# DeltaNet's value transposes as fp32r words beside the fp32 ones, with other banks and another order for the fills of a hybrid decoder block

## The chip, the core and the metric

The kernel runs on one NeuronCore of a Trainium2 chip. Its engines are TensorE (PE in the profile, its weight loads PEld), VectorE (DVE), ScalarE (ACT), GpSimd (POOL) and SyncE (SP), which issues all DMAs here. The metric is device time in microseconds (us) of one execution, median of several; lower is better.

## What is computed

One decoder block on x of 1024 tokens by 1024 features, all in float32. Cut to what matters:

```python
h = rmsnorm(x, norm1_w)
proj = h @ w_in                       # 1024 x 4104, columns split among the groups
# 8 heads of 64: strictly causal stick-breaking attention
#   A[t,s] = sigmoid(z_ts) * prod_{s<j<t} (1 - sigmoid(z_tj)),  o = A @ v
# 4 heads of 128: q, k, v = silu(causal conv of 4 taps); q, k l2-normalised;
#   S_t = exp(g_t) S_{t-1} (I - beta_t k_t k_t^T) + beta_t k_t v_t^T ; o_t = S_t^T q_t
mixed = concat(rmsnorm(o_attention) * silu(z), rmsnorm(o_deltanet) * silu(z'))
x = x + mixed @ w_out
return rmsnorm(x, final_norm_w)
```

The DeltaNet part is computed in chunks, here of 128 tokens: a triangular system per chunk is inverted, and a scan over the eight chunks of a head carries the state.

## The kernel before

**Precision and products.** Large products (input and output projections, attention) split each float32 operand into a high part, written as fp32r, and the remainder, also fp32r, and sum three products (`mm3`, L517: high by high, high by low, low by high). DeltaNet's own small products and all transposes are plain fp32.

**Stages in order of time.** First a straight piece of code: attention's q projection (L563 to L589), while x and the weights are loaded, then the row scales `rstd` (L591 to L600), which go to HBM as `rs_s` and come back to all partitions as `rbc`; DVE multiplies the input by it (L615) and ACT and DVE split it anew into `xh` and `xl` (L647 to L649) while PE computes half of the attention's v and DeltaNet's gate inputs (L641 to L646). Then come the interleaved streams, described below, and in the end the output projection (`product`, L1400).

**Streams.** From L1460 the rest of the program is a set of Python generators (class `Stream`, L378): `projections` (the *fills*: 24 weight column blocks, each in two halves of 512 tokens and 24 matmuls a half, with v's second half of heads among them), `delta_pre`, `delta_load`, `delta_solve` and `delta_scan` for DeltaNet, `attention` with a stream for each window of 256 queries, and the preparation and product of the output projection. `ORDER` (L29) is the order of the fills: G0 (DeltaNet head 0: k, q, v columns), v1, G1, k0 and so on. A generator yields a condition, or an operation whose result its next matmuls need.

**Who goes next.** The kernel simulates itself while it is built. `Model` (L132) gives every recorded operation a cost and an end; `interleave` (L392) takes, whenever PE's modelled queue is empty, the ready stream of the lowest number `prio`; fills have 100 and so go only when no chain is ready. A stream is ready (`Stream.ready`, L386) when each operation that it yielded has ended and its result has had time to reach PE: `HOPS` of its engine plus `TO_PE`, 70 ns. Streams other than fills need one free `pz` bank. The other engines' orders come from the same simulation and are written down as dependencies (L1468 to L1471), so that each engine's order is fixed in the program. PE's is that of the program.

**Banks.** PSUM's eight banks have names: two `pp`, one `pc`, four `pz`, one `po` (L442 to L445). A fill's half waits until one of the two `pp` banks is free (`ps.room`, L839), computes into it, and hands it to an eviction. For DeltaNet columns this is `g_evac` (L775): ACT copies the bank to `pre`, ACT and three DVE operations do the convolution, the first steps in the bank itself, the last into a tile `ac` of tag `kt`, of which there are two; then sigmoid, a POOL product, and a DMA to `g_s`. The evictions for k and z columns use the same two `kt` tiles.

**The part that is changed most.** `gdn_pre` (L920) prepares half a head (four chunks): it transposes k and q (L935), computes norms and the two chunk products (L961), and then, when the values `vt` have been loaded from `g_s` (`delta_load`, L900), transposes the four 128x128 blocks of `vt` into one `pz` bank (L975) and lets ACT copy each, scaled, to `nkv` (L977). The scan (`gdn_chain`, L1091) reads `nkv` later.

**Start.** Eight matmuls of the identity run first on PE (L560), and ACT's first instruction is the scaled copy of the first part of x to `xh` (L578).

Of the kernel before, what the change touches and what calls it, by code (L numbers as in the profile page):

```python
# [10 lines left out]
F32 = mybir.dt.float32  # L11
F32R = mybir.dt.float32r
I32 = mybir.dt.int32
AF = mybir.ActivationFunctionType
# [3 lines left out]
P = 128  # L18
# [20 lines left out]
SAME = 130  # L39
HOPS = {"A": 145, "G": 75, "P": 197, "V": 130, "S": 900}  # L40
TO_PE = 70

PORT = 60

# [87 lines left out]
class Model:  # L132
# [102 lines left out]
    def finish(self, op):  # L235
        op.end = self.now
        for u in op.users:
            self.wake(u, op.end + self.hop(op, u))
        self.at(op.end + HOPS[op.eng] + TO_PE, lambda: None)

    def arrive(self, op):
        if op.late:
# [135 lines left out]
class Stream:  # L378
# [7 lines left out]
    def ready(self, ck):  # L386
        if self.gate and not self.gate():
            return False
        return all(o.end is not None and o.end + HOPS[o.eng] + TO_PE <= ck.now for o in self.waits)


def interleave(ck, room, streams):  # L392
# [29 lines left out]
def block(tc, xT_d, x_d, n1_d, wE_d, wQ_d, wC_d, conv_d, alog_d, dtb_d, mixw_d, wo_d, fnw_d, out_d):  # L422
# [4 lines left out]
    with ExitStack() as top:  # L427
# [33 lines left out]

        make_identity(nc, ident)
        V.memset(step[:, 0:384], 0.0)
        rsg = cst.tile([P, GH, NB], F32, name="rsg")
        gsc = {n: cst.tile([P, GH, NB], F32, name=n) for n in ("beta", "cum", "eg", "neg", "egl", "kd")}

# [90 lines left out]
        alog, dtb = sm[:, 692:696], sm[:, 696:700]  # L557
        qp = [pp(), pp(), pz(), pc(), pz(), pz(), pz(), po()]

        for _ in range(8):  # L560
            TE.matmul(qp[7][:, 0:P], ident, ident, start=True, stop=True)
        raw, loads = [], {"n": [S.dma_start(n1, n1_d)]}
# [236 lines left out]
        def projections():  # L799
# [29 lines left out]
            while nxt:  # L829
                name, cols = nxt  # L830
                if name[0] == "v":
                    nxt = take()
                    split(nxt, 2)
                    yield from values()
                    continue
                fill.prio = 100
                for half in range(2):
                    hs = slice(half * 512, (half + 1) * 512)
                    yield lambda: ps.room("pp", 2)  # L839
                    pt = pp()  # L840
                    for k in range(NK):
                        n = 8 * half + k
                        if n == 2:
                            nxt = take()
                        if n == 8:
                            split(nxt, 1)
                        if n == 12:
                            split(nxt, 2)
                        h, l = cols.hl[k // 4]
                        mm3(pt, h[:, k % 4, :], l[:, k % 4, :], xh[:, k, hs], xl[:, k, hs], k == 0, k == NK - 1)  # L850
                        if k < NK - 1:
                            yield
                    if half == 0:
                        if name[0] == "G":
                            ev = g_evac(int(name[1]), int(name[2]))
                        else:
                            ev = {"k": k_evac, "z": z_evac}[name[0]](int(name[1]))
                    flags[name if half else name + ".0"] = ev(pt, half)
                    yield
                if nxt is None:  # L860
                    nxt = take()
                    if nxt is None and todo:
                        yield lambda: any(ok() for _, ok in todo)
                        nxt = take()
                    split(nxt, 2)
# [15 lines left out]
        def delta_load():  # L881
            yield lambda: "dec" in flags
            for h in range(GH):
                for g in range(2):
                    u = 2 * h + g
                    gst[h, g] = {}
                    half = "" if g else ".0"
                    yield lambda: u < 4 or f"c{u - 4}" in flags
                    if u > 3:
                        yield flags[f"c{u - 4}"]  # L890
                    kq = gd.tile([P, 4, 2, P], F32, tag="kq", bufs=4, name="kq")
                    ts = slice(512 * g, 512 * g + 512)
                    loads = []
                    for kind in (1, 0):
                        yield lambda: f"G{h}{kind}{half}" in flags
                        loads.append(S.dma_start(kq[:, :, 1 - kind, :], g_s[h, kind, :, ts].rearrange("p (c t) -> p c t", c=4)))
                    gst[h, g].update(kq=kq)
                    flags[f"l{u}g"] = loads
                    yield lambda: f"G{h}2{half}" in flags and (u == 0 or f"q{u - 1}" in flags)
                    vt = gd.tile([P, 4, P], F32, tag="vt", name="vt")  # L900
                    flags[f"v{u}g"] = S.dma_start(vt.rearrange("p c t -> p (c t)"), g_s[h, 2, :, ts])
                    gst[h, g].update(vt=vt)

        def delta_solve():
# [15 lines left out]
        def gdn_pre(h, g):  # L920
# [51 lines left out]
            vt = st["vt"]  # L972
            tp = pz()
            for j in range(4):
                TE.transpose(tp[:, j * P:(j + 1) * P], vt[:, j, :], ident)  # L975
            for j in range(4):
                A.activation(nkv[:, j, :], tp[:, j * P:(j + 1) * P], AF.Copy, scale=nk[:, j:j + 1])  # L977
            qg = kq[:, :, 1, :]
            flags[f"q{2 * h + g}"] = G.tensor_tensor(qg, qg, cb, ALU.mult)
            yield  # L980
# [524 lines left out]
```

## Time and profile before

| | |
|---|---|
| median of 3 runs | 667.47 us (667.22 to 668.82) |
| the profiled execution | 667.83 us |
| its span, first to last instruction | 666.1 us |
| mean granted TensorE clock | 0.998 |
| HBM read and written | 75.50 and 34.51 MB |

How to read the rows that follow: a row of a timeline has the start in us, the duration, the engine, the line (L312 is the recorder through which almost every instruction passes, so rows are told apart by their tiles), the operation, the output tile, the input tiles, the shape and the count; in brackets stands the idle time of the engine before it and what ended it. A row of groups has the count, then busy us in all and the mean in ns, then idle us before. Matmul durations overlap, since matmuls are pipelined: how long a series takes is read from the distance of starts. fp32r tiles are shown as f32 in PE rows.

### The profile page before, as it was taken

To read this page: it belongs to the slowest core of one execution; us is meant where nothing else is said; L and a number is where in the kernel's file an instruction comes from. 1 tells how busy PE (TensorE), PEld (TensorE's weight loads), DVE (VectorE), ACT (ScalarE), POOL (GpSimd) and SP (SyncE) were. 2 spreads that over 40 slices of the span, in tenths; PEclk is the share of its full clock that TensorE was granted. 3 is DMA by queue.
4 is the path that set the end of the run, shared out by engine and by line. 5 is a ranking of instruction groups with operands and counts; after the bars stand their busy time and mean duration, and the time that the engine had idled before them with its cause. 6 is when DMAs were issued, how large, how long until landed. Compare 5 with 4: busy or idle time off the path is not lost.

```text
span 666.1 us, 11687 instructions
## 1 busy us (share of the span) xinstructions
PE 654.0 (98%) x3990; PEld 559.1 (84%) x3990; DVE 442.7 (66%) x842; ACT 381.6 (57%) x898; POOL 341.5 (51%) x372
## 2 busy tenths in 40 slices
PE   8999999999999999999999999999999999999996
PEld 6889887998888898888888888788988888888885
DVE  4349984525558989855647786888688952977632
ACT  5636557825447878555548685769697832222111
POOL 0106144918675687726784385823455451665411
PEclk9999999999999999999999999999999999999999
DMA  7929346862674265343692525452546633764411
GB/s 297 333 82 362 115 147 220 292 193 80 213 223 143 71 192 148 102 134 117 173 301 81 179 81 144 136 170 72 164 154 229 198 92 123 245 221 159 136 64 63
DMA packets 96331, 110.78 MB, mean 166 GB/s; under 512 B 29520, under 2 KB 61456, under 8 KB 96272
## 3 DMA queue, kind: packets, MB, share of 16 engines
q1 hardware_dynamic: 96272, 110.04, 51.1%
q8 instruction: 31, 0.51, 0.3%
q14 instruction: 28, 0.23, 0.1%
HBM read 75.50 MB, written 34.51 MB: 165 GB/s over the span
## 4 chain that ended last, share of the span: by engine, by line
PE 81%; DMA 5%; DVE 4%; POOL 3%; ACT 2%; issue 2%; SPq 1%; POOLq 0%; ACTq 0%; DVEq 0%
PE pp L312 47%; PE pz L312 25%; PE po L312 6%; PE pc L312 4%; POOL tt L312 1%; DVE xl L312 1%; DMA wcr<-wC 1%; DMA xa<-xd 1%; DMA dt<-cum_s 1%; DVE xr L312 1%; ACT L312 1%; DMA wer<-wE 1%; SPq L312 1%; DMA cb<-cum_s 1%; POOL wel L312 1%
## 5 line engine op out<-in xcount | busy, mean ns | idle before, releaser
L312 PE MATMUL pp<-xh,weh 128*128 128x512 f32 x384 | 159.3, 415 | 1.4 <-DVE ac L312 1.4
L312 PE MATMUL pp<-xh,wel 128*128 128x512 f32 x384 | 150.7, 392 | 0.3 <-POOL wel L312 0.3
L312 PE MATMUL pp<-xl,weh 128*128 128x512 f32 x384 | 150.2, 391 | 0.3 <-DVE xl L312 0.3
L312 POOL TENSOR_TENSOR sg<-sg,cc 128x128 f32<-128x128 f32 (+3 forms) x64 | 79.1, 1239 | 78.0 <-DVE cc L312 73.9
L312 POOL TENSOR_TENSOR wel<-wer,weh 128x512 fp32r<-128x512 f32 x48 | 61.9, 1292 | 50.2 <-ACT weh L312 49.1
L312 PEld LDWEIGHTS pp<-xh,wel 128*128 128x128 f32 x384 | 72.1, 188 | 16.6 <-POOL wel L312 0.7
L312 PEld LDWEIGHTS pp<-xh,weh 128*128 128x128 f32 x384 | 72.4, 189 | 13.1 <-DVE ac L312 2.0
L312 PEld LDWEIGHTS pp<-xl,weh 128*128 128x128 f32 x384 | 72.5, 189 | 11.4 <-DVE xl L312 0.7
L312 DVE TENSOR_TENSOR al<-pz,ah 128x512 fp32r<-128x512 f32 (+1 forms) x80 | 49.6, 630 | 17.1 <-ACT ah L312 16.7
L312 ACT ACTIVATE sg<-pz,rs 128x384 f32<-128x384 f32 (+3 forms) x96 | 53.7, 589 | 7.5 <-PE pz L312 6.4
L312 DVE TENSOR_TENSOR_SCAN cc<-pz,step 128x384 f32<-128x384 f32 (+2 forms) x64 | 53.3, 846 | 6.4 <-ACT pz L312 6.2
L312 DVE SCALAR_TENSOR_TENSOR pp<-pre,conv,pp 128x512 f32<-128x512 f32 x48 | 35.9, 749 | 30.8 <-ACT pp L312 30.4
L312 ACT ACTIVATE ah<-pz 128x512 fp32r<-128x512 f32 (+1 forms) x80 | 43.8, 558 | 20.8 <-PE pz L312 19.5
L312 ACT ACTIVATE pz<-pz,ns 128x384 f32<-128x384 f32 (+3 forms) x96 | 52.8, 568 | 0.0
L312 POOL TENSOR_TENSOR ac<-ac,pre 128x512 f32<-128x512 f32 x24 | 31.1, 1295 | 29.6 <-ACT pre L312 21.6
L312 PE MATMUL pp<-woh,mh 128*128 128x512 f32 (+2 forms) x120 | 46.1, 384 | 0.0
L312 PE MATMUL pp<-woh,ml 128*128 128x512 f32 (+2 forms) x120 | 45.5, 379 | 0.0
L312 PE MATMUL pp<-wol,mh 128*128 128x512 f32 (+2 forms) x120 | 45.3, 378 | 0.0
L312 PE MATMUL pz<-step,sg 128*128 128x128 f32 x288 | 43.9, 275 | 0.1
L312 PE MATMUL po<-ah,v2a 128*128 128x256 f32 (+1 forms) x160 | 42.8, 292 | 0.0
L312 ACT ACTIVATE xr<-y 128x1024 f32<-128x1024 f32 (+3 forms) x10 | 8.9, 889 | 55.8 <-DVE y L312 55.8
L312 DVE TENSOR_TENSOR_SCAN cc<-pz,cc,step 128x512 f32<-128x512 f32 (+1 forms) x32 | 38.7, 1211 | 3.0 <-ACT pz L312 2.3
(252 smaller groups left out, 1593.4 us busy)
## 6 DMA issues: line engine op xcount, KB each, us to landing
wer<-wE SPq DMA_DIRECT2D x48, 256.0 KB, 3.8
xr<-x SPq DMA_DIRECT2D x16, 512.0 KB, 6.1
g_s<-ac SPq DMA_DIRECT2D x24, 256.0 KB, 2.4
v_s<-v2e SPq DMA_DIRECT2D x16, 256.0 KB, 2.6
kq<-g_s SPq DMA_DIRECT2D x16, 256.0 KB, 3.6
v2a<-v_s SPq DMA_DIRECT2D x8, 512.0 KB, 4.2
q<-qk_s SPq DMA_DIRECT2D x8, 512.0 KB, 5.0
kh<-qk_s SPq DMA_DIRECT2D x8, 512.0 KB, 4.9
```

Of the source, the lines that this page charges most:

```text
L312: ins = f(*args, **kw).ins
```

## The change

1. `SLACK = 450` ns is added to the time at which a stream is ready after an operation that it yielded.
2. A tile `idr` holds the identity as fp32r.
3. ACT's first instruction becomes a copy of the small constant `half` into `rs8` (which is written properly later), ahead of the identity matmuls.
4. The second halves of G0's fills take a `pz` bank instead of a `pp` bank.
5. The tile `vt` becomes fp32r. `gdn_pre` transposes its four blocks as fp32r words into one `pz` bank and once more as fp32 into a second one. DVE copies the fp32 result to a tile `tv` (tag `kt`), subtracts it from the fp32r result into the second bank, and adds 2^30 times this difference to `tv`. ACT's four scaled copies read `tv` instead of PSUM.

```diff
--- before.py
+++ after.py
@@ -39,6 +39,7 @@
 SAME = 130
 HOPS = {"A": 145, "G": 75, "P": 197, "V": 130, "S": 900}
 TO_PE = 70
+SLACK = 450
 
 PORT = 60
 
@@ -236,7 +237,7 @@
         op.end = self.now
         for u in op.users:
             self.wake(u, op.end + self.hop(op, u))
-        self.at(op.end + HOPS[op.eng] + TO_PE, lambda: None)
+        self.at(op.end + HOPS[op.eng] + TO_PE + SLACK, lambda: None)
 
     def arrive(self, op):
         if op.late:
@@ -386,7 +387,7 @@
     def ready(self, ck):
         if self.gate and not self.gate():
             return False
-        return all(o.end is not None and o.end + HOPS[o.eng] + TO_PE <= ck.now for o in self.waits)
+        return all(o.end is not None and o.end + HOPS[o.eng] + TO_PE + SLACK <= ck.now for o in self.waits)
 
 
 def interleave(ck, room, streams):
@@ -461,6 +462,8 @@
 
         make_identity(nc, ident)
         V.memset(step[:, 0:384], 0.0)
+        idr = cst.tile([P, P], F32R, name="idr")
+        V.tensor_copy(idr, ident)
         rsg = cst.tile([P, GH, NB], F32, name="rsg")
         gsc = {n: cst.tile([P, GH, NB], F32, name=n) for n in ("beta", "cum", "eg", "neg", "egl", "kd")}
 
@@ -557,6 +560,7 @@
         alog, dtb = sm[:, 692:696], sm[:, 696:700]
         qp = [pp(), pp(), pz(), pc(), pz(), pz(), pz(), po()]
 
+        A.activation(rs8, half, AF.Copy)
         for _ in range(8):
             TE.matmul(qp[7][:, 0:P], ident, ident, start=True, stop=True)
         raw, loads = [], {"n": [S.dma_start(n1, n1_d)]}
@@ -836,8 +840,9 @@
                 fill.prio = 100
                 for half in range(2):
                     hs = slice(half * 512, (half + 1) * 512)
-                    yield lambda: ps.room("pp", 2)
-                    pt = pp()
+                    wide = name[:2] == "G0" and half
+                    yield lambda: ps.room("pz", 4) if wide else ps.room("pp", 2)
+                    pt = pz() if wide else pp()
                     for k in range(NK):
                         n = 8 * half + k
                         if n == 2:
@@ -897,8 +902,8 @@
                     gst[h, g].update(kq=kq)
                     flags[f"l{u}g"] = loads
                     yield lambda: f"G{h}2{half}" in flags and (u == 0 or f"q{u - 1}" in flags)
-                    vt = gd.tile([P, 4, P], F32, tag="vt", name="vt")
-                    flags[f"v{u}g"] = S.dma_start(vt.rearrange("p c t -> p (c t)"), g_s[h, 2, :, ts])
+                    vt = gd.tile([P, 4, P], F32R, tag="vt", name="vt")
+                    flags[f"v{u}g"] = S.dma_start(vt.rearrange("p c t -> p (c t)").bitcast(F32), g_s[h, 2, :, ts])
                     gst[h, g].update(vt=vt)
 
         def delta_solve():
@@ -972,9 +977,16 @@
             vt = st["vt"]
             tp = pz()
             for j in range(4):
-                TE.transpose(tp[:, j * P:(j + 1) * P], vt[:, j, :], ident)
+                TE.transpose(tp[:, j * P:(j + 1) * P].bitcast(F32R), vt[:, j, :], idr)
+            tq = pz()
             for j in range(4):
-                A.activation(nkv[:, j, :], tp[:, j * P:(j + 1) * P], AF.Copy, scale=nk[:, j:j + 1])
+                TE.transpose(tq[:, j * P:(j + 1) * P], vt[:, j, :].bitcast(F32), ident)
+            tv = pr.tile([P, 512], F32, tag="kt", bufs=2, name="tv")
+            V.tensor_copy(tv, tq)
+            V.tensor_tensor(tq, tp, tv, ALU.subtract)
+            V.scalar_tensor_tensor(tv, tq, 2.0 ** 30, tv, ALU.mult, ALU.add)
+            for j in range(4):
+                A.activation(nkv[:, j, :], tv[:, j * P:(j + 1) * P], AF.Copy, scale=nk[:, j:j + 1])
             qg = kq[:, :, 1, :]
             flags[f"q{2 * h + g}"] = G.tensor_tensor(qg, qg, cb, ALU.mult)
             yield
```

## The prediction

> **What bounds the kernel now.** I read the page's head, then busy time by stage, then the waits of TensorE (PE), then the rows around each longer wait. The stage columns are: length; busy us (instructions) of PE, weight load (PEld), DVE, ACT, POOL; granted clock; DMA share; GB/s.
>
> ```profile
> span 666.1 us, 11687 instructions
> PE 654.0 (98%) x3990; PEld 559.1 (84%) x3990; DVE 442.7 (66%) x842; ACT 381.6 (57%) x898; POOL 341.5 (51%) x372
> ...
> 53.00:82.40 29.40, 29.12 (x218) 27.74 (x216) 28.70 (x33) 16.09 (x25) 12.61 (x6) 1.00 0.67 245
> 82.40:130.00 47.60, 45.48 (x256) 38.88 (x257) 30.22 (x75) 32.76 (x66) 30.34 (x29) 1.00 0.61 215
> ...
> 350.00:541.00 191.00, 190.57 (x1356) 165.52 (x1355) 150.04 (x262) 144.97 (x336) 97.91 (x104) 1.00 0.46 144
> ```
>
> PE bounds the kernel from the first data to the out projection's end: 98% of the span. So a microsecond of PE work added anywhere comes out at the end, and a PE bubble that is closed is gained, unless a later point holds PE back. One such point exists: between 53 and 82.4 us DVE is busy 28.70 of 29.40 us. The profiled execution took 667.83 us, that is 1.7 us around the span of 666.1, and lies 0.36 us above the median of the three runs, 667.47. I sum against 667.83 and take off 0.36 at the end.
>
> **The early activation (first ACT instruction).** In before, ACT's table load comes only when the first input has landed:
>
> ```profile
> 4.25 1.28 ACT L312 ACT_TABLE_LOAD   x1 [4.25 <-DMA xr<-xT]
> 6.32 0.79 PE L312 MATMUL pp<-xh,wqh 128*128 128x512 f32 x1 [1.12 <-ACT xh L312]
> ...
> 37.29 0.69 DVE L312 TENSOR_TENSOR wql<-wq,wqh 128x512 fp32r<-128x512 f32 x1 [0.37 <-ACT wqh L312]
> 38.29 0.38 SPq L312 DMA_DIRECT2D rs_s<-rstd  x1
> 49.01 0.33 SPq L312 DMA_DIRECT2D rbc<-rs_s  x1
> 53.13 1.28 DVE L312 SCALAR_TENSOR_TENSOR xr<-xr,n,rbc 128x1024 f32<-128x1024 f32 x1 [0.24 <-DMA rbc<-rs_s]
> 82.36 0.50 PE L312 MATMUL pp<-xl,weh 128*128 128x512 f32 x1 [0.28 <-DVE xl L312]
> ```
>
> The added instruction waits only for a memset in the first microsecond, so the table is in place before 4.25 and the first `xh` is 1.28 us earlier; PE, which waited 1.12 us for it, starts that much earlier. This isn't what reaches the end. The row scales come back through HBM: `rs_s` is issued at 38.29, `rbc` only at 49.01, and DVE's first multiplication by `rbc` is at 53.13. From there DVE is saturated up to 82.36, where PE waits for `xl`, DVE's last product in the chain. An earlier PE therefore waits longer at 82. What moves this chain is its head: DVE sat 0.37 us waiting for `wqh`, which waits for PE to free its buffer, with the row scales queued behind. I pass on **-0.4 us** of 1.28; the ends are 0 and -1.28.
>
> **The fills' banks.** In before every fill half takes one of two `pp` banks. In G0's stage PE waits for one:
>
> ```profile
> 105.29 0.39 PE L312 MATMUL pp<-xl,weh 128*128 128x512 f32 x1
> 105.52 0.39 PE L312 MATMUL pp<-xh,wel 128*128 128x512 f32 x1
> 107.35 0.50 PE L312 MATMUL pp<-xh,weh 128*128 128x512 f32 x1 [1.44 <-DVE ac L312]
> ...
> PE pp L312 <- DVE v2e L312: 0.7, 2, 0.4
> ```
>
> Fill matmuls start 0.23 us apart (105.29, 105.52), and the last half of G0 starts 1.83 us after the one before it: 1.6 us lost. With second halves in `pz`, halves 2, 4 and 6 hold no `pp` bank, so half 6 finds its bank at once. The value blocks that follow find both `pp` banks free instead of one, and one of the two waits for `v2e` (0.4) goes too; the other stays, as ACT and DVE clear these banks no sooner. Nothing else wants four `pz` banks before the attention begins. **-2.0 us**; ends 0 (if PE, earlier, meets the same evictions later) and -2.3 (1.6 and 0.7).
>
> **The transposes.** Each of the eight half heads gets four more PE transposes.
>
> ```profile
> 128.94 0.60 PE L312 MATMUL pz<-step,vt 128*128 128x128 f32 x4
> ...
> 659.47 0.28 PE L312 MATMUL pp<-wol,mh 128*128 128x192 f32 x1
> 659.58 0.27 PE L312 MATMUL pp<-woh,ml 128*128 128x192 f32 x1
> ...
> 539.86 0.22 PE L312 MATMUL po<-ah,v2a 128*128 128x128 f32 x1
> 539.91 0.28 PE L312 MATMUL po<-al,v2a 128*128 128x128 f32 x1
> L312 PE MATMUL pz<-vr,at 128*128 128x128 f32 x64 | 12.4, 275 | 0.0
> ```
>
> Four fp32 transposes span 0.60 us, of which the last one's own tail is 0.27: three starts in 0.33, 0.11 each. An fp32r transpose isn't in this trace. The nearest row is an fp32r matmul that also loads new weights every time: at 192 columns they start 0.11 apart. Fewer columns aren't quicker then, since at 128 columns an fp32 transpose takes 0.11 too: the load sets it. So 8 x 4 x 0.11 = **+3.5 us**, all on PE, since PE has no idle time to hide it in. Lower end: 0.05 as between the two products with `v2a` at 539.86, which use the same weights, so +1.6. Upper end: two passes, as the plain fp32 matmuls show (32 `vr,at` products in the code, 64 in the trace), so 0.22 each and +7.0.
>
> The Trainium skill ("TensorE: Matmul & The Clock Gate", section "Weight-path perf modes — Fast Weight Load (FWL) and DoubleRow") says that a load of 128 weights is sped up by itself when the type isn't FP32. Were fp32r such a type, the sum would be 1.9 us lower; the 0.11 at 192 columns of fp32r speaks against it.
>
> **What hangs on the transposes.** DVE gets a copy, a subtraction and a fused multiply-add of 128x512 per half head; ACT's four scaled copies read SBUF instead of PSUM.
>
> ```profile
> L312 DVE COPY kn<-pz 128x512 f32<-128x512 f32 x8 | 5.5, 687 | 9.4 <-ACT nkv L312 9.4
> L312 DVE TENSOR_TENSOR al<-pz,ah 128x512 fp32r<-128x512 f32 x48 | 32.3, 684 | 12.4 <-ACT ah L312 12.1
> L312 DVE SCALAR_TENSOR_TENSOR pp<-pre,conv,pp 128x512 f32<-128x512 f32 x48 | 35.9, 749 | 30.8 <-ACT pp L312 30.4
> L312 ACT ACTIVATE nkv<-pz,nk 128x128 f32<-128x128 f32 x32 | 9.1, 368 | 10.8 <-PE pz L312 10.8
> 214.22 0.49 PE L312 MATMUL pc<-nkv,xinv 128*128 128x128 f32 x2
> ```
>
> That is 0.69 + 0.68 + 0.75 = 2.1 us, 17 us of DVE in all, put at nothing on the path: DVE is off it (150.04 of 191 us in the attention's long stage), and `nkv` is early, made at 129 and first used by the scan at 214.22. Its cover would be gone where a scan already waits for `nkv`, or where a fill's eviction does for what is queued behind these three; the price is the second slower rival below. The `idr` copy stands in the idle first microseconds of DVE. The two banks held instead of one are of four, for some 3 us, eight times.
>
> **SLACK.** A stream now goes on only 450 ns after the time at which the scheduler's model has its releaser arrive at PE; fills are put there instead. PE then meets fewer values that aren't ready. PE's weight loads between 130 and 560 us show what they waited for (us in total, times, longest):
>
> ```profile
> PEld pz L312 <- DVE cc L312: 3.6, 12, 0.6
> ...
> PEld pz L312 <- ACT o L312: 1.4, 6, 0.4
> ...
> PEld pc L312 <- DVE xct L312: 0.5, 3, 0.2
> PEld pz L312 <- DVE v L312: 0.5, 3, 0.2
> ```
>
> `o`, `xct` and `v` are values that a stream yields for, so SLACK reaches them: 2.4 us in 12 waits. A load waits partly beside the matmul in flight, some 0.1 us each (the start distance of the short ones above): **-1.2 us**. `cc` is a bank that is used again, and banks are tested without SLACK. Ends: -2.4, and above nothing if the delayed chains end late (the first slower rival). No engine's queue gets a wait by it: it changes the order alone.
>
> **Sum.** -0.4 - 2.0 + 3.5 - 1.2 = -0.1 us: 667.83 becomes 667.7, and beside the median **667.4 us**. Within 0.3% (2.0 us), about what a measurement of this kernel can tell from no change.
>
> **Rivals.**
>
> *Faster, 665.0 us: later chains also free the banks.* If each chain comes later, a `pz` bank's last reader has more often finished when it is used again; then the 12 waits for `cc` go too, 3.6 - 12 x 0.1 = 2.4 us. For it: `cc` is the longest of the loads' waits. Against: the test for a free bank is unchanged.
>
> *On the edge of faster, 665.5 us: fp32r loads are quick at 128 columns.* 0.05 instead of 0.11 each, 1.9 us less. Against: the rows at 659.47.
>
> *Slower, 670.9 us: fp32r transposes take two passes*, 3.5 us more. Against: the fp32 ones take one.
>
> *Slower, 676.7 us: SLACK outlasts the fills.* Chains are stretched, and fills are used up sooner. At the end of attention only fills are left, one piece in the chain of work that ended last (start, us, what):
>
> ```profile
> 541.15 17.72 PE pp L312 x78
> ```
>
> That is 17.7 us of cover. By the code each attention head has 19 waits on values (loads, and 3 to 6 in each of four windows), 0.45 us each; six heads run after 350 us. Three windows abreast it is 18/3 x 0.45 + 0.45 = 3.2 us a head, 19 us: just the cover. Two abreast it is 4.5 us a head, 27 us, and PE idles 9.3 us. It decides at about 3 us a head. Against: out-projection products of DeltaNet's half can fill in first.
>
> *Slower, 671.6 us: the new tile takes a fill's buffer.* `tv` takes one of two `kt` slots, which the fills' evictions write. It is held over the copy, subtraction, add and four ACT copies: 2.1 + 4 x 0.37 = 3.6 us. A half lasts 24 x 0.23 = 5.5 us and its eviction has three DVE passes of 0.75, so 3.3 us are spare at most; less two ACT passes, of at least 0.37 each, 2.6 are left, and a late slot costs PE 1.0 us. At half of the eight it is 4.2 us. Against: most fills then are interleaved with other PE work, and so last longer.
>
> **How the numbers follow.** Forecast 0.36; banks freed 0.22, quick loads 0.08; two passes 0.10, fills outlasted 0.10, buffer taken 0.14. The quick loads lie on the bound and count half to each side of it: faster 0.26, same 0.40, slower 0.34. The range leaves out the far rival (0.10) and some of both tails: 663.5 is the banks' case with wide and start at their better ends, 672.0 takes in the buffer and the two passes.
>
> **What would show it.** Start: the table load before 2 us, the first PE product near 5.0, and a wait for `xl` near 82 that has grown to over 1 us; if PE passes `xl`'s end more than 1 us sooner than at 82.36, this step is wrong. Banks: no wait for `ac` in G0. Transposes: starts of `vt` groups 0.11 apart; 0.05 or 0.22 would make that term wrong. SLACK: fewer waits of loads for `o`, `xct`, `v`; PE still full from 541 to 650. Buffer: waits of `pp` for `ac` near the groups of `vt`. The forecast falls if PE has idle stretches after 500 us, or if the loads' waits for `cc` go.

## The result and the profile after

The changed kernel takes 671.68 us (median of 4 runs, 671.01 to 672.22) against 668.03 us (667.22 to 668.82, 4 runs) for the kernel before: a ratio of 1.0053, 95% interval 1.0037 to 1.0069. A second comparison on another chip gave 1.0037 (1.0015 to 1.0059). The change costs 0.4 to 0.5%, 3 to 4 us (the medians differ by 3.7 and 3.6). The forecast, 667.4 us and "within 0.3%", was too low; 671.68 lies inside its range, near the upper end.

The head of the page of after, and its busy time by stage (columns as in the prediction, which has the same windows of before):

```profile
span 669.5 us, 11742 instructions
PE 657.8 (98%) x4022; PEld 561.0 (84%) x4022; DVE 459.9 (69%) x867; ACT 381.8 (57%) x899; POOL 342.1 (51%) x372
```

```profile
82.40:130.00 47.60, 47.60 (x287) 42.33 (x286) 28.69 (x75) 32.51 (x64) 30.01 (x29) 1.00 0.63 215
350.00:541.00 191.00, 190.45 (x1325) 163.61 (x1325) 150.69 (x260) 139.44 (x339) 101.14 (x107) 1.00 0.44 137
```

PE is still the bound, with 3.8 us more busy time (657.8, 654.0 before) in a span 3.4 us longer. A second profile of the same kernel (e_after_again) has 656.5 us of busy PE in a span of 669.6, so busy time is good to a microsecond or so. Between 82.4 and 130 us it now has no idle time (45.48 of 47.60 before): what the banks were to bring is there. It is given back later.

**The start.** Timeline rows of after:

```profile
0.79 1.28 ACT L313 ACT_TABLE_LOAD   x1 [0.79 <-PEq L1492]
...
5.43 0.80 PE L313 MATMUL pp<-xh,wqh 128*128 128x512 f32 x1 [0.23 <-ACT xh L313]
...
82.08 0.50 PE L313 MATMUL pp<-xl,weh 128*128 128x512 f32 x1 [0.30 <-DVE xl L313]
...
105.17 0.39 PE L313 MATMUL pz<-xh,weh 128*128 128x512 f32 x1
```

The table load stands at 0.79 instead of 4.25, and the first product starts 0.89 us earlier. The lead is 0.50 us at 12 us already and stays so until DVE's last `xl`, where 0.28 us of it is left (82.08 against 82.36). The wait for `xl` is 0.30 us, 0.28 before. The last half of G0, at 105.17 in `pz`, waits for nothing; the wait of 1.44 us for `ac` is gone. G0's last matmul starts at 110.4 us, 112.7 before.

**The transposes.** The instructions of `vt` and `tv` by tile (durations in ns: least, median, greatest), and one group in the timeline:

```profile
L313 PEld LDWEIGHTS pz<-idr,vt x32: 137/140/145, 128.7 to 371.0; 128*128 128x128 f32 x32
L313 PE MATMUL pz<-idr,vt x32: 222/247/414, 128.7 to 371.0; 128*128 128x128 f32 x32
L313 PEld LDWEIGHTS pz<-step,vt x32: 137/141/143, 129.2 to 371.3; 128*128 128x128 f32 x32
```

```profile
L313 ACT ACTIVATE nkv<-tv,nk x32: 385/388/418, 133.2 to 377.6; 128x128 f32<-128x128 f32 x32
L313 DVE SCALAR_TENSOR_TENSOR tv<-pz,tv x8: 679/688/692, 132.2 to 375.3; 128x512 f32<-128x512 f32 x8
```

```profile
186.31 0.46 PE L313 MATMUL pz<-idr,vt 128*128 128x128 f32 x4
186.60 0.62 PE L313 MATMUL pz<-step,vt 128*128 128x128 f32 x4
```

There are 32 of the fp32r transposes, so one pass each. A group of four moves the next one back by about 0.3 us (186.31 to 186.60); inside the groups the median distance of starts is 0.08 us (0.057 to 0.249 over the 24 pairs). DVE and ACT take about what the forecast took (688 ns for the multiply-add, 388 for a scaled copy).

**The waits.** PE's own waits in after, and its weight loads between 130 and 560 us (us in total, times, longest):

```profile
PE pz L313 <- DVE cc L313: 1.1, 2, 0.9
PE pc L313 <- POOL ml L313: 0.8, 1, 0.8
...
PE pp L313 <- POOL ml L313: 0.3, 1, 0.3
```

```profile
PEld pz L313 <- DVE cc L313: 6.5, 20, 1.1
...
PEld pc L313 <- DVE xct L313: 0.2, 1, 0.2
PEld pz L313 <- DVE v L313: 0.2, 1, 0.2
```

The loads' waits for `o`, `xct` and `v`, 2.4 us in 12 before, are down to 0.4 in two: SLACK reached what it was expected to reach. But the loads' waits for `cc`, which the forecast left as they were, grew from 3.6 us in 12 to 6.5 in 20, and PE itself has two new places of idleness, at 277 and 573 us:

```profile
278.18 0.66 PE L313 MATMUL pz<-step,vt 128*128 128x128 f32 x4 [0.93 <-DVE cc L313]
```

```profile
574.53 0.50 PE L313 MATMUL pc<-woh,ml 128*128 128x512 f32 x1 [0.79 <-POOL ml L313]
```

The first is the second bank of the values' transposes: the fp32 group, which follows the fp32r group of 276.61, starts only when DVE has read `cc` out of it. The second lies at the start of the out projection, where before had no wait at all; the forecast had named idle PE after 500 us as a sign that it falls. In the chain of work that ended last PE is left out for 8.6 us there:

```profile
563.77 2.10 PE pp L313 x9
...
565.95 0.60 ACT zs L313
566.55 1.05 ACT woh L313
567.62 1.08 DVE wol L313
...
571.58 0.64 ACT mh L313
572.30 2.19 POOL ml L313
574.53 2.59 PE pc L313 x10
```

PE has DeltaNet's half of the out projection to work on meanwhile, but not enough of it. The attention's last `o` is transposed 18.7 us later than in before, with 24 fill matmuls still to come instead of 99 (one row of before, one of after):

```profile
540.77 0.38 PE L312 MATMUL pz<-step,o 128*128 128x128 f32 x2
...
559.50 0.38 PE L313 MATMUL pz<-step,o 128*128 128x128 f32 x2
```

### The profile page after: what moved, and what is told of

Read it like the earlier page. It is cut to its first block, busy times and chain, and to the rows that moved or that the text cites. A ratio compares the mean times of both kernels' runs of the same rounds, so it can differ in the third digit from the quotient of the medians.

```text
span 669.5 us, 11742 instructions
## 1 busy us (share of the span) xinstructions
PE 657.8 (98%) x4022; PEld 561.0 (84%) x4022; DVE 459.9 (69%) x867; ACT 381.8 (57%) x899; POOL 342.1 (51%) x372
## 4 chain that ended last, share of the span: by engine, by line
PE 80%; DVE 7%; POOL 4%; ACT 3%; DMA 3%; issue 2%; SPq 0%; POOLq 0%; DVEq 0%; ACTq 0%
PE pp L313 46%; PE pz L313 25%; PE po L313 6%; PE pc L313 3%; POOL tt L313 2%; DVE cc L313 1%; DVE xl L313 1%; DMA wcr<-wC 1%; POOL wel L313 1%; DMA wer<-wE 1%; DVE xr L313 1%; DMA xb<-xe 0%; DMA xr<-xT 0%; ACT pz L313 0%; DVE al L313 0%
## 5 line engine op out<-in xcount | busy, mean ns | idle before, releaser
L313 PE MATMUL pp<-xh,weh 128*128 128x512 f32 x360 | 151.8, 422 | 0.0
L313 PE MATMUL pp<-xh,wel 128*128 128x512 f32 x360 | 141.5, 393 | 0.3 <-POOL wel L313 0.3
L313 PE MATMUL pp<-xl,weh 128*128 128x512 f32 x360 | 141.1, 392 | 0.3 <-DVE xl L313 0.3
L313 PEld LDWEIGHTS pp<-xh,wel 128*128 128x128 f32 x360 | 67.6, 188 | 15.9 <-POOL wel L313 0.7
L313 PEld LDWEIGHTS pp<-xl,weh 128*128 128x128 f32 x360 | 68.1, 189 | 10.0 <-DVE xl L313 1.1
L313 PEld LDWEIGHTS pp<-xh,weh 128*128 128x128 f32 x360 | 67.9, 189 | 9.6 <-DVE ac L313 0.5
L313 DVE SCALAR_TENSOR_TENSOR pp<-pre,conv,pp 128x512 f32<-128x512 f32 x42 | 31.5, 750 | 24.2 <-ACT pp L313 23.7
L313 PE MATMUL po<-al,v2a 128*128 128x256 f32 (+1 forms) x160 | 39.2, 281 | 0.0
```

What stands on the lines that cost most here:

```text
L313: ins = f(*args, **kw).ins
```

## The experiments

To add up where PE's time goes, I worked out one figure from each trace: for every pair of neighbouring matmuls the usual distance of their starts (the 30th percentile over all pairs of that trace with the same shapes and types, fp32 or fp32r, and the same shape and type ahead of them), and by how much each pair exceeds it. Excesses over 20 ns, summed by stage, are called PE's lost time below (us, of the one profiled execution):

| kernel | span | fills after the last `o` | lost to 20 us | 20-130 | 130-545 | after 545 | span less lost |
|---|---|---|---|---|---|---|---|
| before | 666.1 | 99 | 5.3 | 3.9 | 6.6 | 0.0 | 650.3 |
| after | 669.5 | 24 | 4.8 | 0.9 | 9.1 | 1.7 | 653.0 |
| e_front_slack | 664.6 | 42 | 4.3 | 2.4 | 7.4 | 0.0 | 650.5 |
| e_fixed_order | 668.2 | 99 | 5.0 | 4.4 | 6.6 | 0.0 | 652.2 |
| e_kept_no_fp32r | 667.8 | 24 | 3.0 | 2.2 | 9.6 | 2.0 | 651.0 |
| e_kept_no_values | 667.8 | 24 | 3.0 | 2.7 | 8.9 | 2.3 | 650.9 |

The last column is the work itself: 650.3 to 651.0 us without fp32r transposes, 652.2 and 653.0 with them; the two pairs of the same order differ by 1.9 (before and e_fixed_order) and 2.0 (e_kept_no_fp32r and after). The rest of each span is lost time, and where it is lost differs from order to order. How it is shared between the first two stages differs from run to run too: e_after_again, the kernel after once more, loses 2.7 and 3.0 us there instead of 4.8 and 0.9, the same 5.7 in sum.

The theories that the expectations name: **A**, the parts add up, each by its own mechanism, SLACK with a cost of its own by delaying the attention. **B**, the waits that DVE's three operations and the banks of the values' transposes bring are the cost; **B2**, it is the second group of transposes with its second bank. **C**, every edit gives the scheduler another order, and that scatters the time whatever the edit is. **D**, the transposes cost their PE time, and all else is the order.

**One part each.** Three kernels each make one part of the change in the kernel before, and a fourth makes all but the values' part.

e_front (the early activation and G0's banks):

```diff
+        A.activation(rs8, half, AF.Copy)
...
-                    yield lambda: ps.room("pp", 2)
-                    pt = pp()
+                    wide = name[:2] == "G0" and half
+                    yield lambda: ps.room("pz", 4) if wide else ps.room("pp", 2)
+                    pt = pz() if wide else pp()
```

> The kernel before with the early activation and the pz banks of G0's second halves only (no SLACK, values transposed as before). In the trace of the changed kernel the value blocks end 2.9 us sooner than before although two half heads' extra transposes (0.32 us each) lie ahead of them. Theory A (the parts add up: front -3.5, transposes +2.6 on PE and +1 in a wait for a bank, SLACK +3.5): 3 to 3.5 us faster than before, about 664.7. Rival B (the transposes' DVE work and banks cost far more, SLACK costs nothing): the same here. Rival C (every new order of the program scatters the time by some us): within 2 us of before either way.

Measured: 1.0035 (1.0015 to 1.0055), 672.37 us against 669.49. Slower, where the parts alone should have gained. Its profile is the slowest of its 12 runs (675.92 us). G0 does end earlier there (its last matmul starts at 110.9, before 112.7), but the value blocks end later (143.7, before 142.9). PE's longest waits:

```profile
PE pz L312 <- ACT nkv L312: 2.5, 1, 2.5
PE pp L312 <- DVE v2e L312: 2.0, 1, 2.0
PE pp L312 <- DVE ac L312: 1.9, 1, 1.9
```

Before had 0.7 us for `v2e`, 1.4 for `ac` and none for `nkv`. The wait for `v2e` ends at 122.64, in the value blocks, that for `nkv` at 278.38, that for `ac` at 337.57: they are at other places than before's. At 123.3 the granted clock also falls to half for 3.4 us, which costs PE 1.7 us; without that the value blocks would have ended at about 142.0, earlier than before's (see "The clock beside the long waits").

e_slack (SLACK alone):

```diff
+SLACK = 450
...
-        self.at(op.end + HOPS[op.eng] + TO_PE, lambda: None)
+        self.at(op.end + HOPS[op.eng] + TO_PE + SLACK, lambda: None)
...
```

> The kernel before with SLACK = 450 only. Theory A: slower by about 3.5 us, 671.5: the attention's last output transposes move from 541 to near 560 us, the output projection meets waits for ml of some 1.5 us at its start, and the loads' waits for cc do not fall. Rival B: within 1 us of before, or up to 1 us faster, with the attention's end as in before. Rival C: any sign, and a time that does not follow from the attention's end.

Measured: 0.9974 (0.9957 to 0.9991), 667.96 against 669.49. The attention's last `o` comes at 553.0, 12 us later than in before, and no time is lost at the out projection: 42 fill matmuls are left. By itself SLACK does what was forecast and more: of the loads' 12 waits for `o`, `xct` and `v` one is left (0.2 us), and those for `cc` fall from 3.6 to 2.3 us.

e_transposes (the values' part alone):

```diff
+                TE.transpose(tp[:, j * P:(j + 1) * P].bitcast(F32R), vt[:, j, :], idr)
...
+            V.tensor_copy(tv, tq)
+            V.tensor_tensor(tq, tp, tv, ALU.subtract)
+            V.scalar_tensor_tensor(tv, tq, 2.0 ** 30, tv, ALU.mult, ALU.add)
```

> The kernel before with the values' fp32r transposes, tv and idr only. Theory A: slower by 2.6 us of PE work (8 x 0.32) and up to 1 us of waits: 670.6 to 671.6. Rival B: slower by 5 to 7 us, 673 to 675, with the attention's end late by over 10 us. Rival C: anywhere from 668 to 674.

Measured: 1.0052 (1.0034 to 1.0070), 673.29 against 669.49: 3.5 us. Without any SLACK the attention's last `o` comes at 557.1, 16 us later than in before.

e_front_slack (the changed kernel without the values' part; shown against after):

```diff
-            V.tensor_copy(tv, tq)
-            V.tensor_tensor(tq, tp, tv, ALU.subtract)
...
-                A.activation(nkv[:, j, :], tv[:, j * P:(j + 1) * P], AF.Copy, scale=nk[:, j:j + 1])
+                A.activation(nkv[:, j, :], tp[:, j * P:(j + 1) * P], AF.Copy, scale=nk[:, j:j + 1])
```

> The changed kernel with the values transposed as before (early activation, pz banks and SLACK = 450 stay). Theory A: -3.5 + 3.5, so within 1 us of before, 668; attention still ends near 560. Rival B: 664 to 665, since nothing that costs is left; attention ends near 541. Rival C: no sum of the single parts.

Measured: 0.9951 (0.9934 to 0.9967), 666.42 against 669.49: faster than both kernels, by 3.3 us than before. What follows from the four: the front costs 0.35%, SLACK gains 0.26%, and the two together gain 0.49%. Parts don't add up, so A falls in this form; and the values' part costs 0.9 to 1.0% in one surrounding and 0.5% in the other.

**One piece of the values' part out of after.** All four ran on one chip.

e_after_again (no edit):

> The changed kernel once more, beside the three below on one chip, as their base: 0.5% over before, as measured first. Theory A now (SLACK and the fills' banks together gain what was forecast for them; what costs is the values' part, 2.6 us on PE itself and as much again in the attention's delay beyond the fills' cover): attention's last output transposes near 560, waits for ml of 1 to 2 us at the start of the output projection. Rival C (each new order scatters the time): the same.

Measured: 1.0037 (1.0015 to 1.0059), 671.94 against 668.38.

e_no_tv (DVE's three operations and `tv` removed; ACT reads the fp32 result from PSUM, and the fp32r result is read by nobody):

```diff
-            V.tensor_copy(tv, tq)
...
-                A.activation(nkv[:, j, :], tv[:, j * P:(j + 1) * P], AF.Copy, scale=nk[:, j:j + 1])
+                A.activation(nkv[:, j, :], tq[:, j * P:(j + 1) * P], AF.Copy, scale=nk[:, j:j + 1])
```

> The changed kernel without tv: the fp32r transposes are made and nobody reads them, ACT scales the fp32 transposes from PSUM as before; left out are the copy, the difference and its addition. Theory A: the PE work alone, 2.6 us over the kernel without the values' part (0.9951 of before), so 0.9990 of before; attention ends within 3 us of 552 and no wait for ml. Rival B2 (the second transposes themselves break the order, DVE's part is harmless): 1.003 or more.

Measured: 1.0092 (1.0061 to 1.0124), 675.26. Less work, and slower than after: PE waits 3.4 us for `wol` at 583.66, with 87 fill matmuls left after the last `o`.

e_no_fp32r (no fp32r transposes; DVE's work stays, on the fp32 result alone):

```diff
-                TE.transpose(tp[:, j * P:(j + 1) * P].bitcast(F32R), vt[:, j, :], idr)
...
-            V.tensor_tensor(tq, tp, tv, ALU.subtract)
+            V.tensor_tensor(tq, tq, tv, ALU.subtract)
```

> The changed kernel without the fp32r transposes: DVE's copy, subtraction (of the fp32 transposes from themselves) and multiply-add stay, with tv in a kt slot. Theory A: DVE's 17 us and the tile cost the other half, 1.000 to 1.002 of before, with the attention's end near 558 and a wait for ml. Rival B2: as the kernel without the values' part, 0.995 to 0.996.

Measured: 1.0057 (1.0035 to 1.0079), 672.82.

e_no_kt (`tv` is made in `nkv`'s own space, so no slot of `kt` is taken):

```diff
-            tv = pr.tile([P, 512], F32, tag="kt", bufs=2, name="tv")
+            tv = nkv.rearrange("p c d -> p (c d)")
```

> The changed kernel with the copy, difference and addition made in the tile nkv itself, so that no kt slot is taken; ACT scales nkv in place. Forecast's rival of the buffer: 4 us of the changed kernel's time go, 0.999 of before. Theory A: DVE's work, not the slot, delays: within 1 us of the changed kernel, 1.004 to 1.006.

Measured: 1.0149 (1.0117 to 1.0180), 679.15, the slowest of all. None of the removals gained anything, so B and B2 get no support; but each kernel has another order, with its long waits at other places, so they don't refute them either. For instance e_no_kt's longest PE waits:

```profile
PE po L313 <- DVE al L313: 4.8, 2, 4.4
PE pz L313 <- DVE xq L313: 2.3, 1, 2.3
```

**The order held still.** From here on either the order is kept and the work changes, or the work is kept and the order changes. In e_fixed_order the 32 fp32r transposes are put into the kernel before without the scheduler's knowledge, into the bank that the fp32 ones then overwrite; every engine otherwise keeps its order (in the traces, the same rows in the same sequence, but for one memset of DVE in e_fixed_order_fs). e_fixed_order_fs is the same in e_front_slack.

```diff
-                TE.transpose(tp[:, j * P:(j + 1) * P], vt[:, j, :], ident)
+                nc.tensor.transpose(tp[:, j * P:(j + 1) * P].bitcast(F32R), vt[:, j, :], idr)
+            for j in range(4):
+                TE.transpose(tp[:, j * P:(j + 1) * P], vt[:, j, :].bitcast(F32), ident)
```

> The kernel before with the 32 fp32r transposes alone, put in without the scheduler's knowledge: they go into the bank that the fp32 transposes then overwrite, and the order of every engine stays that of before, instruction for instruction. Left out are tv, the difference and everything that reads the fp32r words. Theory D (the transposes cost their PE time, 8 x 0.32 = 2.6 us; all else that the single parts showed is the new order that each of them brings): 1.0039 of before, within 0.8 us. Theory A (the second transposes hold up DeltaNet or the attention by more than their PE time): 1.006 or more. Forecast's rival of two passes: 1.010.

> The same 32 transposes in the order of the kernel with early activation, pz banks and SLACK but values as before (0.9951 of before). Theory D: 0.9951 + 0.0039 = 0.999 of before; with the scheduler's knowledge of them the same instructions gave 1.0092. Theory A: about 1.009 here too.

Measured: 1.0029 (1.0010 to 1.0047), 670.70 against 668.41, and 0.9982 (0.9962 to 1.0002), which is 0.0031 above 0.9951. Both say the same: 32 fp32r transposes cost 2 us or a little more (0.0029 x 668.4 = 1.9; the medians differ by 2.3), with nothing but PE time behind it:

```profile
span 668.2 us, 11752 instructions
...
PE 656.3 (98%) x4022; PEld 561.5 (84%) x4022; DVE 440.3 (66%) x843; ACT 382.6 (57%) x898; POOL 341.6 (51%) x372
```

PE's busy time is 2.3 us over the 654.0 of before, and its lost time is 16.0 us, 15.8 before.

**The work held still.** Six kernels have exactly the instructions of before, of e_front_slack or of after, and one constant of the scheduler's model moved:

```diff
-SAME = 130
+SAME = 135
...
-TO_PE = 70
+TO_PE = 75
...
-SLACK = 450
+SLACK = 440
```

> The kernel before, the same instructions, with one constant of the scheduler's model changed by 4% (SAME from 130 to 135 ns): another order and nothing else. Theory D: the order before is a lucky one among its neighbours, so this is slower by 1 to 6 us (1.002 to 1.009), by a few single waits of over 0.5 us in places that have to do with no edit. Theory A: within 1 us of before.

> The kernel before with TO_PE 75 instead of 70 ns in the scheduler's model, nothing else. Theory D: slower by 1 to 6 us, 1.002 to 1.009. Theory A: within 1 us of before.

> The kernel with early activation, pz banks and SLACK, values as before, with SLACK 440 instead of 450. Theory D: a few us from its neighbour at 450 (0.9951), slower more likely than faster, 0.996 to 1.004. Theory A: SLACK is worth its 450 within 1 us, 0.995 to 0.997.

> Early activation, pz banks and SLACK 460, values as before. Theory D: 0.996 to 1.010, between its neighbours at 450 (0.9951) and 440 (1.011) or beyond; no slope from 440 to 460 is expected. A rival, that SLACK has a sharp best value: 0.995 to 0.998, with 440 just below a threshold.

> The changed kernel with SLACK 440 instead of 450: the same instructions in another order. Theory D: the changed kernel's own order is one draw of many, so this lies a few us to either side of it (1.0037 to 1.0053 of before): 1.002 to 1.014. Theory A: within 1 us of the changed kernel.

> The same with SLACK 460. Theory D: 1.002 to 1.014, not the time of 440. Theory A: within 1 us of the changed kernel.

| kernel | edit | ratio to before (95%) |
|---|---|---|
| e_reroll_before | SAME 135 | 1.0037 (1.0013 to 1.0061) |
| e_reroll_before_75 | TO_PE 75 | 1.0015 (0.9989 to 1.0041) |
| e_reroll_fs | SLACK 440, no values' part | 1.0110 (1.0077 to 1.0142) |
| e_reroll_fs_460 | SLACK 460, no values' part | 0.9955 (0.9939 to 0.9970) |
| e_reroll_after_440 | SLACK 440 | 1.0079 (1.0053 to 1.0104) |
| e_reroll_after_460 | SLACK 460 | 1.0071 (1.0046 to 1.0096) |

So the same instructions in another order move by up to 1.6% (0.9951 to 1.0110), and 0.37% when a model constant moves by 5 ns (with `TO_PE` 75 the 0.15% isn't clear of noise). A difference of 0.5% between two orders doesn't tell, then, what an edit costs. The waits of e_reroll_before are an example; PE waits longer for `wel` and `v2e`, where before had 0.3 and 0.7 us:

```profile
PE pp L312 <- POOL wel L312: 2.4, 2, 1.3
PE pp L312 <- DVE v2e L312: 2.3, 1, 2.3
```

e_reroll_fs shows the far end of the rival "SLACK outlasts the fills": the attention's last `o` is at 566.0, after the last fill (560.4), and PE waits at the out projection, until 577.0 and 627.9 us (the profile is the slowest of six runs, 679.79 us, median 676.18):

```profile
PE pc L313 <- ACT mh L313: 3.8, 1, 3.8
PE pp L313 <- POOL ml L313: 2.3, 1, 2.3
```

**The clock beside the long waits.** Part of the scatter between the profiles isn't the waits themselves. In e_reroll_fs the granted TensorE clock falls to half while PE waits for `mh`, and stays there for 6.8 us (the columns are those of the stages; the clock is the third value from the end):

```profile
575.50:582.40 6.90, 5.25 (x12) 3.67 (x13) 5.45 (x10) 1.86 (x3) 4.80 (x4) 0.51 0.63 189
```

The products of 512 columns start 0.43 us apart then (580.24, 580.67), 0.23 from 582.37 on. Such stretches, of 3.4 or 6.8 us, begin during a wait of PE or at most about 1 us after one in e_front (two), e_no_fp32r (two), e_no_tv (one), e_no_kt (two), e_reroll_fs (two), e_reroll_after_440 and e_reroll_after_460 (one each); while PE has work they cost it 1.7 us for each 3.4. Outside the first 15 us and the last 7 there is none in before, after, e_front_slack, e_fixed_order and the two kernels that follow, so the comparisons of these are free of it. A wait as long needn't bring one: the 2.27 us for `v2e` in e_reroll_before, which end at 119.07, don't. How long a wait it takes isn't shown.

**After's own order, with the values' work taken out.** The last two kernels settle what after's loss consists of. The values' part is planned as in after, so that every engine keeps after's order, but part of it is not issued.

```diff
-                TE.transpose(tp[:, j * P:(j + 1) * P].bitcast(F32R), vt[:, j, :], idr)
+                a = (tp[:, j * P:(j + 1) * P].bitcast(F32R), vt[:, j, :], idr)
+                ck.record("P", None, [a[0]], list(a[1:]), cost("P", "transpose", a, {}), None)
...
```

e_kept_no_fp32r leaves out the fp32r transposes in this way and subtracts the fp32 result from itself; e_kept_no_values leaves out DVE's three operations too, and ACT's copies read PSUM.

> The changed kernel in its own order on every engine, without the 32 fp32r transposes: they are planned, so that the scheduler makes the same order, and not issued; the subtraction takes the fp32 result minus its own copy, so the term that is added is zero. The changed kernel gave 1.0053 and 1.0037 of before. Theory D (the transposes cost their PE time, 2.3 to 2.6 us as in the kernels whose order was kept, and the rest of the loss is the new order): 0.0035 to 0.0039 less, 1.001 (0.999 to 1.003). If the transposes also bring waits of their own in this order: 0.999 or less. If they hide in waits that come anyway: 1.003 or more.

> The changed kernel in its own order, without the 32 fp32r transposes and without the three DVE operations of each half head (planned, not issued); ACT's scaled copies read the fp32 result from PSUM, at their old places. What is left is the start, G0's banks, SLACK and the order. Theory D: the same as the kernel that leaves out the transposes alone, 1.001, within 0.0015; then the order by itself costs 0.006 (4 us) beside the 0.9951 of the start, the banks and SLACK in the order that they have without the values' part. Rival (the DVE work and its banks cost time): 0.9951 to 0.998, at least 0.002 below that kernel; then the order costs nothing.

Measured: 1.0019 (0.9992 to 1.0047), 670.50 against 668.56, and 1.0004 (0.9978 to 1.0029), 669.68. The heads of both pages, first without the fp32r transposes, then also without DVE's work:

```profile
span 667.8 us, 11671 instructions
...
PE 655.1 (98%) x3990; PEld 557.2 (83%) x3990; DVE 460.9 (69%) x867; ACT 382.0 (57%) x899; POOL 341.7 (51%) x372
```

```profile
span 667.8 us, 11647 instructions
...
PE 654.9 (98%) x3990; PEld 557.2 (83%) x3990; DVE 446.2 (67%) x843; ACT 380.9 (57%) x899; POOL 341.7 (51%) x372
```

DVE's work is 14.7 us less (460.9 to 446.2) and the span is the same; the ratios differ by 0.0015, inside their intervals. After minus the transposes is 0.0018 to 0.0034 (1.0037 and 1.0053 less 1.0019), 1.2 to 2.3 us. What remains, 1.0004, is the start, the banks and SLACK in after's order. The same parts in e_front_slack's order gave 0.9951; the two traces have the same rows on every engine, 3990 on PE, in another sequence. So the order alone, with the choice of `pz` banks that comes with it, costs 0.53%, 3.5 us (by the two intervals 1.5 to 5.6). The rival (DVE's work and its banks cost, the order nothing: at most 0.998) falls by the measured value, though the lower end of the interval just touches it.

The table of lost time says where: the two spans differ by 3.2 us, and 2.3 us of it are lost after 545 us, where e_front_slack loses nothing; 1.5 us more are lost between 130 and 545 us, where the loads' waits for `cc` are 5.2 us instead of 2.3. After 545 us the chain of e_kept_no_values is that of after, 2.3 us earlier (`woh` at 564.21, `ml` at 569.96, PE at 572.20).

ACT's rows at that place, of e_front_slack and then of after, show what stands ahead of `mh` and `ml`:

```profile
563.24 1.14 ACT L313 ACTIVATE woh<-wor,mixw 128x1024 fp32r<-128x1024 f32 x1
564.28 1.14 ACT L313 ACTIVATE mh<-mf 128x512 fp32r<-128x512 f32 x2
565.32 3.22 ACT L313 ACTIVATE woh<-wor,mixw 128x1024 fp32r<-128x1024 f32 x3
```

```profile
566.44 2.18 ACT L313 ACTIVATE woh<-wor,mixw 128x1024 fp32r<-128x1024 f32 x2
569.33 1.15 ACT L313 ACTIVATE woh<-wor,mixw 128x1024 fp32r<-128x1024 f32 x1 [0.70 <-DMA wor<-wo]
571.58 1.23 ACT L313 ACTIVATE mh<-mf 128x512 fp32r<-128x512 f32 x2 [1.10 <-DVE mf L313]
```

`mh` waits for DVE's `mf`. DVE's rows, of e_front_slack and then of after:

```profile
563.12 0.56 DVE L313 TENSOR_TENSOR mf<-pz,gt 128x384 f32<-128x384 f32 x1 [3.98 <-PE pz L313]
...
564.41 1.29 DVE L313 SCALAR_TENSOR_TENSOR wol<-wor,mixw,woh 128x1024 fp32r<-128x1024 f32 x1
```

```profile
567.62 2.48 DVE L313 SCALAR_TENSOR_TENSOR wol<-wor,mixw,woh 128x1024 fp32r<-128x1024 f32 x2 [0.35 <-ACT woh L313]
...
570.80 0.55 DVE L313 TENSOR_TENSOR mf<-pz,gt 128x384 f32<-128x384 f32 x1
```

In the fast order `mh` comes after one split of the output weights on ACT, and DVE makes `mf` ahead of `wol`; in after `mh` comes behind three splits, and `mf` behind two `wol`. The attention ended 7 us later (559.5, 552.2), so at that time the mix wasn't ready, and the scheduler filled ACT and DVE with weight splits. POOL's `ml` itself takes 2.18 us there, 1.30 in the median of its four, with another `wol` on DVE at 572.06; how the wait of 0.79 us divides between the late start and the longer `ml` wasn't tested.

## Why the prediction was wrong, point by point

Two slips of the text itself change nothing: the lower end of the range is 663.8 by its own terms (665.0 less 0.3 and 0.9), not 663.5, and where it says the first and the second slower rival it means the fills outlasted and the buffer taken.

**The early activation: the start right, the gain not shown.** The table load and the first product moved as described. But the wait for `xl`, which should have grown to over 1 us, is 0.30 us: the lead was down to 0.50 us at 12 us, long before the point that PE can't pass. The 0.28 us left there (0.4 forecast) can't be told from chance: PE passes the last `xl` at 82.4 to 83.4 us in the six profiles without the early activation and at 81.7 to 84.0 in the fourteen with it.

**The fills' banks: right in place, not in worth.** In both profiles of after the wait for `ac` in G0 is gone, PE loses 5.7 us up to 130 us instead of 9.2, and the last matmul of the value blocks starts at 140.0 instead of 142.9, -2.9 us where start and banks had -2.4 forecast. But the gain at the end holds for this order only: e_front, with the same banks, has other long waits and is slower than before.

**The transposes: the mechanism right, the size too large.** All on PE without cover, one pass: shown by e_fixed_order. Forecast 3.5 us; measured 2.3 us by the medians and by busy time (by the ratio's interval 0.7 to 3.1), 1.9 and 2.0 in the column of work of the two pairs in the same order. The nearest row, the fp32r matmuls at 192 columns 0.11 apart, was too dear: the starts lie 0.08 apart in the median. The rival of quick loads (0.05 each) was half true. Of the Trainium skill's rule cited there ("TensorE: Matmul & The Clock Gate", section "Weight-path perf modes — Fast Weight Load (FWL) and DoubleRow"), the trace shows nothing in the recorded lengths of the loads, 140 ns for fp32r and 141 for fp32; their starts lie 0.086 us apart in the median for fp32r and 0.109 for fp32.

**What hangs on the transposes: right for DVE in after's order, open for the second bank.** DVE's work, 14.7 us by busy time, costs nothing that can be measured in a kept order (spans of 667.8 both). The sign of the rival of the `kt` slot (0.14) isn't in after, which has no wait for `ac`. It is in a neighbour: in e_reroll_after_440 PE waits 2.23 us for `ac` at 281.40, after a group of `vt` at 270.42 whose three DVE operations (272.06 to 275.00) stand ahead of that fill's convolution (276.46 to 281.35); whether the slot or DVE's queue held it wasn't tested. The second bank, costed at nothing, stopped PE once, 0.93 us at 278.18; but the two kept kernels, without the fp32r group and this wait, lose as much between 130 and 545 us (9.6 and 8.9, after 9.1), so it isn't shown to cost.

**SLACK: the step that failed.** It was put at -1.2 us, because "it changes the order alone", and an order was taken to cost nothing by itself. The 12 waits for `o`, `xct` and `v` did go, but for two, as forecast. But from 130 us on PE loses 10.8 us (9.1 + 1.7) instead of 6.6, +4.2 where -1.2 was forecast: the waits for `cc`, taken as fixed, grew, and the out projection waits. With -3.5 up to 130 us and +2.7 in the column of work, 2.0 of it the transposes, that makes the +3.4 us of the span. By the times, the three terms without the transposes, -3.6 in sum, came to +0.3 in after's order (1.0004, 0.9978 to 1.0029). The order is not SLACK's alone: the values' part, the banks and SLACK each change it, and it is one outcome of all three. SLACK in e_slack and e_front_slack did gain; without the values' part the sum of the other terms, -3.6, was close to the measured -3.3, but after e_reroll_fs (1.0110) that agreement counts as luck as much as proof.

**The rival that came nearest: "SLACK outlasts the fills".** The attention was delayed by 18.7 us, where the rival had worked out 19, against a cover of 17.7. It was at its point of decision, and PE lost 1.7 us rather than 9.3, since DeltaNet's half of the out projection filled in, as the rival's own counter-argument said. Its cause was put too narrowly: e_transposes without SLACK delays the attention by 16 us as well, and e_reroll_before_75, with none of the edits, by 21. And few fills left are not enough for a loss: e_reroll_before_75 has 12 left and loses 0.1 us after 545, with one split ahead of `mh` as in e_front_slack, and e_reroll_after_460 has 24 left like after and loses nothing there.

**What stays open:** whether SLACK gains on an average over orders (0.9951 and 0.9955 against 1.0110 is no average), and why after's neighbours at 440 and 460 are 0.2 to 0.4% slower still. Their profiles show the half clock for 3.4 us in each, 1.7 us of PE time, and at 440 the wait for `ac`; but single runs of the two with a mean clock of 0.999 took 674.66 and 675.19 us, no less than the others, so the clock isn't shown to be the reason. That the late attention leads the scheduler to put the splits ahead is read from the traces; a kernel that forces `mh` ahead of them in after's order wasn't run.

## What to carry to other kernels

Where a scheduler with a model makes a static order, measure first how far the time moves when a constant of the model moves and the work stays: here 0.4% for 5 ns in one, and 1.6% between neighbours of another, so that a forecast made of costs alone can't be better than that. To price a piece of work, keep the order of every engine and add or omit the piece; to price an order, keep the work. When waits of some microseconds come into play, read the granted clock beside them: here it fell to half after several, which made them dearer. And when a chain is delayed up to the end of its cover, look at what the other engines do in the meantime: the work that moves forward into the gap (here weight splits) then stands ahead of what the bound engine waits for.

## What the runs showed of the hardware

An fp32r transpose of 128x128 that loads its own weights starts 0.08 us after the one before it (median of 24 pairs in after), against 0.11 for the fp32 transpose and for the fp32r matmul at 192 columns, although the recorded load is as long (140 and 141 ns). In eleven places of seven profiles the granted clock was halved for 3.4 or 6.8 us with a wait of PE beside it, and products of 512 columns started 0.43 us apart instead of 0.23.
